# Two-block network on one core: fourteen modulation sums moved out of the keys-and-values stage into the attention blocks, by halves, and the transposes of the context's roots moved two row tiles ahead

## The chip, the cores and the metric

One Trainium2 chip, of which the program uses 1 core. The time is device microseconds of one execution; lower is better. It was taken in three runs before the change, and one further execution was recorded by the profiler.

## The reference, cut to what matters

The network has two blocks. The part that the change touches is the first layer of the first block, attention over 512 latent tokens and 256 context tokens, and the modulation vector that feeds it:

```python
m_lat = (s_c @ ada_w[l] + ada_b[l])[:, None, :]          # 6*1024 sums over 1024
sh1, sc1, g1, sh2, sc2, g2 = jnp.split(m_lat, N_MOD, axis=-1)
h_lat = modulate(rms_norm(x, mix_norm[l]), sh1, sc1)
h_ctx = modulate(rms_norm(ctx, mix_norm[l]), csh1, csc1)
y_lat, y_ctx = attention_mixer(h_lat, h_ctx, ...)
x = x + g1 * y_lat
x = x + g2 * conv_ffn(modulate(rms_norm(x, ffn_norm[l]), sh2, sc2), ...)
...
# attention_mixer: keys and values of context and latent tokens side by side
p = (p1 - lam * p2)                     # 4 differential heads, two softmaxes each
oa = rms_norm(einsum(p, v), subln) * (1 - lam_init)
ob = gqa_attend(rms_norm(qb), rms_norm(kb), vb)          # 8 grouped query heads
```

`sh1` and `sc1` are wanted before attention; `g1`, `sh2` and `sc2`, of which the change moves sums, only after it.

## The kernel before, in words

All products are done in float32 split into a high and a low part, so each product of two tiles is three matmuls (lines 205 to 207); the high part is written by ScalarE (line 160, `wh`, `kh`, `vah`, `reg`, `pth`), the low part by VectorE (lines 163 and 169, `wl`, `kl`, `val`, `ptl`). Weights arrive as `raw` tiles of 128x1024 through the queue of SyncE, two buffers deep in this stage, and are split into one of three `wh`/`wl` pairs.

A modulation vector of 1024 is eight columns of 128 in `mod`. Each column is one load of a 128x1024 tile `ada` (512 KB) and one VectorE instruction, a product with the vector `silu_c` and a sum along the row (line 454, shown as CUSTOM_DVE_ANT_0, followed by a read of the accumulator).

The stages around the change, in the order of the program:

- **Row tiles** (`attention1_start`): a schedule written out by hand for all engines. For each of eight row tiles of x, VectorE and ScalarE write `h` (lines 1054 to 1057), then TensorE multiplies what is there with six weight tiles (`tiles`, two in single banks `b1`, four in the two double banks `b2`). At k == 4 VectorE works out the roots of the context's mean squares (`A`, tile `spread`); at k == 7 TensorE transposes them into `Rc`, a piece of bank `side`. After the eight tiles VectorE forms the context's rows from `cx` and `Rc`.
- **Keys and values** (`attention1`, up to `self.lam()`): rope of four query tiles and two key tiles (lines 714 to 717), the stores of keys, the products for values (`v_copy`, `v_all`) and for three more key tiles, each for latent and context tokens (`kv_gemm`). `more(2)` puts two modulation sums after each step, fourteen in all, with two `ada` buffers. There are two single banks; a product waits until VectorE and ScalarE have read the bank's last content. `lam()` loads a small vector on ScalarE's queue (`lv`), sums it on VectorE and takes an exponential on ScalarE (line 989). In this stage the builder's scheduler sets each engine's order; engines work their queues in that order.
- **Blocks of attention**: the order of TensorE is written out by hand, the others follow the scheduler. Blocks 0 to 15 are those of the differential heads, with two score products, two maxima (`nm`, line 910), two exponentials (`e`, line 914) and two GpSimd instructions (lines 964 and 965) each; blocks 16 to 47 are those of the grouped heads, with one of each and no GpSimd. Two blocks later the weights are transposed (line 926) and split (`pth`, `ptl`), then multiplied with the values. Between them, `fill()` puts steps of the remaining projections: four query tiles in bank `side` (`q_norm_steps`), with their norms on VectorE (`hn_v`, `hn_y`, `rsq_b`, `spread`, `hn`) and, once, the norm and store of the last key tile `k` through two `e` tiles. There are four `e` tiles, and scores have two double banks, freed by the exponential.
- **Output** (`attention1_out`): the remaining ten sums of the layer, unchanged.

Of the kernel before, what the change touches and what calls it, by code (L numbers as in the profile page):

```python
# [9 lines left out]
F32 = mybir.dt.float32  # L10
# [3 lines left out]
ALU = mybir.AluOpType  # L14
# [4 lines left out]
P = 128  # L19
# [100 lines left out]
class Net:  # L120
# [331 lines left out]
    def ada_tile(self, pool, l, m, tag, bufs):  # L452
        r = self.ada_raw(pool, l, m, tag, bufs)
        self.nc.vector.tensor_tensor_reduce(  # L454
            out=r, in0=r, in1=self.silu_c, scale=1.0, scalar=self.col("ada_b", 48 * l + m), op0=ALU.mult, op1=ALU.add,
            accum_out=self.mod[:, l, m:m + 1])

    def ada_start(self, rows, pairs):

# [535 lines left out]
    def attention1_start(self, es, hc):  # L995


        nc = self.nc
# [4 lines left out]
        with self.tc.manual_schedule(engines=FULL_ORDER):  # L1003
# [70 lines left out]
            for k in range(KD):  # L1074
                r = rows(x[k], k, 0, R, h[0][k], h[1][k])
# [27 lines left out]
                if k == 4:  # L1103
                    A = root(stc, 1024.0)
                next(s)
                if k == 7:
                    self.spread_rows(A, 2, Rc)

                for z in tiles:
# [8 lines left out]
            for k in range(KD):  # L1118
                c = tuple(self.t(hc, [P, NCTX], F32R, f"c{n}{k}") for n in "hl")
                self.hctx.append(c)  # L1120
                r = rows(cx[:, k, :], k, 1, Rc, *c)
# [12 lines left out]
    def attention1(self):  # L1134
        nc = self.nc
        with ExitStack() as es:
# [3 lines left out]
            with ExitStack() as e0:  # L1140
                hc = self.adap = self.pool(e0, "hc")
                with ExitStack() as e1:
                    qs, ks = self.attention1_start(e1, hc)
                kvp = self.pool(e0, "kvp")
                inp = self.pool(es, "inputs", side="right")
                ada = iter(range(16, 40))

                def more(n):
                    for _ in range(n):
                        self.ada_tile(kvp, 0, next(ada), "ada", 2)  # L1150

                for s, z in enumerate(ks):
                    self.k_store(kvp, *z, s, nc.vector)
                    more(2)
                vt = self.v_copy(kvp, 13)
                more(2)
                self.v_all(kvp)
                more(2)
                for s, w in enumerate((5, 7)):
                    self.k_store(kvp, *self.kv_gemm(w), 2 + s, nc.vector)  # L1160
                    more(2)
                self.v_store(kvp, vt, 4)
                more(2)
                key = [self.t(inp, [P, 768], F32, "k16"), self.t(kvp, [P, 768], F32, "vt", 1)]
                bc, bl = self.kv_gemm(12)
                self.gained(None, bc, self.col("k_norm"), None, 0, key[0][:, 0:NCTX], key[1][:, 0:NCTX])
                squares = self.gained(None, bl, self.col("k_norm"), None, 0, key[0][:, NCTX:], key[1][:, NCTX:])[2]
                hv = self.t(self.tiny, [P, 28], F32, "hn_v", 2)
                self.mean_sq(hv[:, 16:28], key[1], 64.0, 1e-6, self.sel2)
                with self.tc.issue_after(squares.ins):  # L1170
                    self.lam()
            ap = self.adap = self.pool(es, "attn")
# [7 lines left out]
            q, k, v, es_, pts = {j: [] for j in range(6)}, {}, {}, {}, {}  # L1180
# [34 lines left out]
            with self.tc.manual_schedule(engines=PE_ORDER):  # L1215
                for n in range(max(due) + 2):
                    if n < len(blocks):
                        m, i, qt = blocks[n]
# [12 lines left out]
                        pts[due[n]] = pt  # L1231
                    if n < len(blocks):
                        rest()
                    if n == 40:
                        hn = self.new_h(0)
                    if 40 <= n < 46:
# [3 lines left out]
                    if j % 2:  # L1240
                        m, i, qt = blocks[j]
                        at = slice((qt - 1) * P, (qt + 1) * P)
# [618 lines left out]
```

## Time and profile before

| | |
|---|---|
| median of 3 runs | 3438.53 us (3437.78 to 3439.02) |
| profiled execution, its own time | 3439.95 us |
| its span, first to last instruction | 3438.2 us |
| TensorE busy (share of the span) | 3323.4 us (97%) |
| VectorE busy | 1994.2 us (58%) |
| ScalarE busy | 1379.2 us (40%) |
| GpSimd busy | 291.6 us (8%) |
| mean granted TensorE clock | 0.986 |

Times in the trace are microseconds from the span's start. PE is TensorE, DVE VectorE, ACT ScalarE, POOL GpSimd, SP SyncE. The change lies in the first 400 us; from 394 us on TensorE is busy for 2992.31 of 3044 us. The idle time before an instruction is given in brackets with what ended it; where the engine named had long been done, it was another.

### The profile page before, as it was taken

The page shows a single profiled execution, that of the slowest core. Times are in us where ns is not written, and L with a number is a line of the kernel's source. Part 1 is how long each engine was busy: PE and PEld are TensorE (multiplying, and loading weights), DVE is VectorE, ACT ScalarE, POOL GpSimd, SP SyncE. Part 2 cuts the span into 40 slices and gives each one's busy share as a digit, 9 for nine tenths or more (in the row PEclk, how much of TensorE's full clock was granted, in tenths as well). Part 3 has the DMA queues.
Part 4 walks back from the last instruction along what each step waited for, and adds up shares of the span by engine and source line. Part 5 has one row for each costly group of instructions (what it writes and reads, how often), then busy time and mean ns, then how long its engine had stood idle before and what let it go on. Part 6 is the DMA issues. An engine that isn't in the chain of part 4 may idle for free.

```text
span 3438.2 us, 43735 instructions
## 1 busy us (share of the span) xinstructions
PE 3323.4 (97%) x17013; PEld 2847.3 (83%) x17013; DVE 1994.2 (58%) x3406; ACT 1379.2 (40%) x2085; POOL 291.6 (8%) x341
## 2 busy tenths in 40 slices
PE   8878999999999999999999999999999999899998
PEld 7767798888888889888888888898888888788887
DVE  6777887766574555333776533363333699873335
ACT  3246643334353343222485522242222466552222
POOL 0052000000000000000222100020000222220001
PEclk9989999999999999999999999999999999999999
DMA  5731456643232323222222323245222133133231
GB/s 196 244 109 34 181 167 204 206 144 102 74 104 98 99 84 104 95 97 93 76 93 89 105 97 98 93 136 185 97 94 93 50 104 99 43 119 98 91 101 47
DMA packets 126209, 381.74 MB, mean 111 GB/s; under 512 B 13745, under 2 KB 28209, under 8 KB 125874
## 3 DMA queue, kind: packets, MB, share of 16 engines
q1 hardware_dynamic: 125282, 377.77, 33.9%
q8 instruction: 134, 2.20, 0.3%
q10 hardware_dynamic: 720, 1.18, 0.1%
q14 instruction: 73, 0.60, 0.1%
HBM read 360.54 MB, written 18.35 MB: 110 GB/s over the span
## 4 chain that ended last, share of the span: by engine, by line
PE 85%; DVE 6%; ACT 4%; issue 3%; DMA 2%; POOL 1%; SPq 0%; ACTq 0%; DVEq 0%; POOLq 0%
PE b L205 23%; PE b L207 23%; PE b L206 23%; PE side L205 2%; PE b L88 1%; PE bo L942 1%; PE side L206 1%; PE side L207 1%; PE b L85 1%; PE b L86 1%; PE b L926 1%; DVE wl L163 1%; PE s L834 1%; PE s L833 1%; DVE nm L910 1%
## 5 line engine op out<-in xcount | busy, mean ns | idle before, releaser
L205 PE MATMUL b<-reg,wh 128*128 128x512 f32 (+1 forms) x3841 | 1435.5, 375 | 16.1 <-ACT wh L160 5.6
L206 PE MATMUL b<-reg,wh 128*128 128x512 f32 (+1 forms) x3841 | 1435.5, 374 | 2.3 <-DVE reg L163 2.3
L207 PE MATMUL b<-reg,wl 128*128 128x512 f32 (+1 forms) x3841 | 1434.6, 374 | 0.5 <-DVE wl L163 0.5
L160 ACT ACTIVATE wh<-raw 128x1024 fp32r<-128x1024 f32 (+2 forms) x549 | 559.7, 1026 | 1318.0 <-PE b L206 1178.8
L163 DVE TENSOR_TENSOR wl<-raw,wh 128x1024 fp32r<-128x1024 f32 (+2 forms) x549 | 653.2, 1195 | 557.8 <-ACT wh L160 549.0
L205 PEld LDWEIGHTS b<-reg,wh 128*128 128x128 f32 x3841 | 727.1, 189 | 145.3 <-ACT wh L160 6.0
L206 PEld LDWEIGHTS b<-reg,wh 128*128 128x128 f32 x3841 | 727.1, 189 | 129.7 <-DVE reg L163 2.7
L207 PEld LDWEIGHTS b<-reg,wl 128*128 128x128 f32 x3841 | 726.8, 189 | 128.9 <-DVE wl L163 1.0
L696 DVE TENSOR_TENSOR sg<-sg,b 128x512 f32<-128x512 f32 x88 | 60.4, 688 | 283.2 <-PE b L207 275.3
L617 POOL TENSOR_TENSOR accs<-x,x 128x512 f32<-128x512 f32 x6 | 10.3, 1709 | 2447.3 <-DVE x L615 2447.3
L1695 DVE SCALAR_TENSOR_TENSOR x<-b,x 128x512 f32<-128x512 f32 x64 | 44.3, 692 | 190.1 <-PE b L207 190.1
L85 PE MATMUL b<-reg,wh 128*128 128x256 f32 x496 | 126.8, 288 | 7.1 <-ACT reg L656 6.5
L86 PE MATMUL b<-reg,wl 128*128 128x256 f32 x496 | 124.8, 284 | 0.0
L530 ACT ACTIVATE sq<-x 128x256 f32<-128x256 f32 (+1 forms) x111 | 51.6, 472 | 162.9 <-DVE x L608 88.0
L160 ACT ACTIVATE reg<-sg 128x512 fp32r<-128x512 f32 x132 | 83.1, 630 | 73.2 <-DVE sg L701 70.9
L454 DVE CUSTOM_DVE_ANT_0 ada<-ada,silu_c,cols 128x1024 f32<-128x1024 f32 x80 | 99.2, 1280 | 12.4 <-DMA ada<-ada 12.4
L160 ACT ACTIVATE pth<-b 128x384 fp32r<-128x384 f32 (+1 forms) x160 | 82.0, 534 | 59.1 <-PE b L926 56.4
L205 PE MATMUL side<-reg,wh 128*128 128x512 f32 x221 | 98.1, 444 | 6.2 <-DVE hn L755 3.9
L85 PEld LDWEIGHTS b<-reg,wh 128*128 128x128 f32 x496 | 95.5, 192 | 9.2 <-ACT reg L656 8.4
L163 DVE TENSOR_TENSOR ptl<-b,pth 128x384 fp32r<-128x384 f32 (+1 forms) x160 | 94.5, 603 | 14.5 <-ACT pth L160 13.5
L163 DVE TENSOR_TENSOR reg<-sg,reg 128x512 fp32r<-128x512 f32 x132 | 90.3, 685 | 18.2 <-ACT reg L160 18.2
L926 PE MATMUL b<-ident,e 128*128 128x128 f32 x544 | 83.4, 282 | 15.2 <-DVE ptl L163 7.9
(356 smaller groups left out, 4031.1 us busy)
## 6 DMA issues: line engine op xcount, KB each, us to landing
raw<-up SPq DMA_DIRECT2D x264, 512.0 KB, 3.4
ada<-ada SPq DMA_DIRECT2D x88, 512.0 KB, 5.0
raw<-down SPq DMA_DIRECT2D x96, 448.0 KB, 3.3
raw<-down SPq DMA_DIRECT2D x48, 512.0 KB, 3.3
raw<-q SPq DMA_DIRECT2D x24, 512.0 KB, 3.4
raw<-rg_in SPq DMA_DIRECT2D x20, 512.0 KB, 3.3
raw<-attn_in SPq DMA_DIRECT2D x14, 512.0 KB, 5.8
raw<-rg_out SPq DMA_DIRECT2D x16, 320.0 KB, 3.0
```

The source lines that it names most:

```text
L85: mm(out=b[:, sl], lhsT=w[0][:, k, :], rhs=h, start=k == 0, stop=False)
L86: mm(out=b[:, sl], lhsT=w[1][:, k, :], rhs=h, start=False, stop=False)
L160: return self.nc.scalar.activation(out=hi, in_=src, func=AF.Copy, scale=scale)
L163: return self.nc.vector.tensor_tensor(out=lo, in0=src, in1=hi.bitcast(F32), op=ALU.subtract)
L205: mm(out=ps, lhsT=ah, rhs=bh, start=first, stop=False)
L206: mm(out=ps, lhsT=ah, rhs=bl, start=False, stop=False)
L207: mm(out=ps, lhsT=al, rhs=bh, start=False, stop=last)
L454: self.nc.vector.tensor_tensor_reduce(out=r, in0=r, in1=self.silu_c, scale=1.0, scalar=self.col("ada_b", 48 * l + m), op0=ALU.mult, op1=AL ...
L530: self.nc.scalar.activation(out=s, in_=x, func=AF.Square)
L696: nc.vector.tensor_tensor(out=sg, in0=sg, in1=bu, op=ALU.mult)
L926: nc.tensor.transpose(out=b[:, i * P:(i + 1) * P], in_=e[:, (k0 + i) * P:(k0 + i + 1) * P], identity=self.ident)
L1695: self.nc.vector.scalar_tensor_tensor(out=x[m], in0=b, scalar=c, in1=x[m], op0=ALU.mult, op1=ALU.add)
```

## The change

The call `more(2)` goes, and with it the fourteen sums after the steps of keys and values. A new helper loads half a column's tile (128x512, 256 KB) and sums it; the second half starts from the first one's result, and there is one buffer. The source places one half in each block n from 17 to 44, 28 halves. The transposes of the context's roots go from k == 7 to k == 5.

```diff
+    def ada_half(self, pool, l, m, half):
+        r = self.t(pool, [P, 512], F32, "ada", 1)
+        at = slice(512 * half, 512 * half + 512)
+        nc.sync.dma_start(out=r, in_=self.a["ada"][48 * l + m][:, at])
+        acc = self.mod[:, l, m:m + 1]
+        nc.vector.tensor_tensor_reduce(out=r, in0=r, in1=self.silu_c[:, at], scale=1.0,
+                                       scalar=acc if half else self.col("ada_b", 48 * l + m), op0=ALU.mult, op1=ALU.add, accum_out=acc)
...
-                if k == 7:
+                if k == 5:
                     self.spread_rows(A, 2, Rc)
...
-                def more(n):
-                    for _ in range(n):
-                        self.ada_tile(kvp, 0, next(ada), "ada", 2)
...
                 for s, z in enumerate(ks):
                     self.k_store(kvp, *z, s, nc.vector)
-                    more(2)
                 vt = self.v_copy(kvp, 13)
-                more(2)
                 self.v_all(kvp)
-                more(2)
                 for s, w in enumerate((5, 7)):
                     self.k_store(kvp, *self.kv_gemm(w), 2 + s, nc.vector)
-                    more(2)
                 self.v_store(kvp, vt, 4)
-                more(2)
...
                     if n < len(blocks):
                         rest()
+                    if 17 <= n < 45:
+                        if n % 2:
+                            part = next(ada)
+                        self.ada_half(ap, 0, part, 1 - n % 2)
```

Lines from 464 on carry a number ten higher after the change, in `attention1` too up to the removed calls. What the builder makes of it, at three places:

TensorE in the row tiles: `ident,spread` are the two transposes of the context's roots, `reg` the rows of h, `silus,ada` the last small products of the modulation. Before, 60 rows after these products:

```order
L205 MATMUL b_82_210<-reg_5_52_141,ada_544 128x512
L206 MATMUL b_82_210<-reg_13_60_149,ada_544 128x512
L207 MATMUL b_82_210<-reg_5_52_141,ada_545 128x512
L382 MATMUL side_153<-ident_78,spread_467 128x128 x2
L205 MATMUL b_104_292<-reg_6_53_142,wh_288 128x512
```

and after it, directly behind them:

```order
L206 MATMUL b_81_209<-reg_11_58_147,wh_411 128x512
L207 MATMUL b_81_209<-reg_3_50_139,wl_412 128x512
L494 MATMUL bo_154<-silus_157,ada_484 128x2 x8
L382 MATMUL side_153<-ident_78,spread_467 128x128 x2
L205 MATMUL b_104_292<-reg_4_51_140,wh_288 128x512
```

The transposes moved ahead of the products of row tiles 4 and 5.

ScalarE at the end of keys and values: `k` and `vt` are the copies of the last key tile's banks (128x512 latent, 128x256 context), `lv` the load of lam's vector, `misc` its exponential, `e` the first softmax. Before:

```order
L731 ACTIVATE k_262_1271<-b_267_1279,cols_76 128x512
L732 ACTIVATE vt_1272<-b_267_1279 128x512
L983 DMA lv_1342<-lam 128x256
L160 ACTIVATE wh_1524<-raw_1522 128x1024
L731 ACTIVATE k_262_1271<-b_268_1280,cols_76 128x256
L732 ACTIVATE vt_1272<-b_268_1280 128x256
L989 ACT_TABLE_LOAD
L989 ACTIVATE misc_90<-misc_90 128x2
L914 ACTIVATE e_1396,zs_1365<-b_293_1389,nm_1394 128x768
```

and after:

```order
L741 ACTIVATE k_248_1229<-b_253_1237,cols_76 128x512
L742 ACTIVATE vt_1230<-b_253_1237 128x512
L993 DMA lv_1300<-lam 128x256
L999 ACT_TABLE_LOAD
L999 ACTIVATE misc_90<-misc_90 128x2
L160 ACTIVATE wh_1482<-raw_1480 128x1024
L741 ACTIVATE k_248_1229<-b_254_1238,cols_76 128x256
L742 ACTIVATE vt_1230<-b_254_1238 128x256
L924 ACTIVATE e_1354,zs_1323<-b_279_1347,nm_1352 128x768
```

The exponential of lam moved ahead of a weight's split and of the two context copies.

VectorE in block 7 of the differential heads: `nm` are its two maxima, `rsq_b`, `hn_y` and `spread` the last Newton step of the norms and its spreading, `rz` a softmax's weight. Before:

```order
L362 SCALAR_TENSOR_TENSOR rsq_b_1682<-rsq_b_1682,hn_v_1333 128x28
L163 TENSOR_TENSOR ptl_1739<-b_389_1746,pth_1738 128x3x128
L363 SCALAR_TENSOR_TENSOR hn_y_1681<-rsq_b_1682,hn_y_1681 128x28
L962 RECIPROCAL rz_1754<-z_1729 128x1
L747 COPY spread_1779<-hn_y_1681 128x256
L963 SCALAR_TENSOR_TENSOR rz_1754<-rz_1754,zs_1365,misc_90 128x1
L910 TENSOR_REDUCE nm_1802<-b_399_1797 128x1
L910 TENSOR_REDUCE nm_1811<-b_403_1806 128x1
```

and after:

```order
L920 TENSOR_REDUCE nm_1760<-b_385_1755 128x1
L973 SCALAR_TENSOR_TENSOR rz_1712<-rz_1712,zs_1323,misc_90 128x1
L363 SCALAR_TENSOR_TENSOR hn_y_1639<-rsq_b_1640,hn_y_1639 128x28
L465 ISA ada_2816,mod_86<-ada_2816,silu_c_159,mod_86 128x512
L465 ISA mod_86 128x1
L920 TENSOR_REDUCE nm_1769<-b_389_1764 128x1
L361 TENSOR_TENSOR rsq_b_1640<-hn_y_1639 128x28
L362 SCALAR_TENSOR_TENSOR rsq_b_1640<-rsq_b_1640,hn_v_1291 128x28
L363 SCALAR_TENSOR_TENSOR hn_y_1639<-rsq_b_1640,hn_y_1639 128x28
L757 COPY spread_1737<-hn_y_1639 128x256
```

A half (the two ISA rows) stands between the two maxima, and the spread moved from ahead of both maxima to behind them. VectorE's queue is not in the hand-written order, and the scheduler puts the first half behind block 0 and the last one into block 18.

## Rows read from the trace of the kernel before

**Rows 1.** Busy time by stretch: us, busy of each engine, granted clock, DMA share, GB/s.

```profile
85.86:176.00 90.14, 79.87 (x394) 67.81 (x394) 62.03 (x101) 24.21 (x37) 0.00 (x0) 0.92 0.81 249
176.00:205.00 29.00, 26.01 (x141) 22.30 (x142) 17.66 (x34) 17.36 (x36) 14.05 (x8) 0.94 0.42 127
205.00:245.00 40.00, 24.02 (x133) 20.55 (x132) 35.97 (x64) 17.02 (x38) 23.88 (x15) 0.80 0.27 79
245.00:276.00 31.00, 30.26 (x177) 26.53 (x177) 18.43 (x32) 17.33 (x37) 18.48 (x12) 0.93 0.28 77
276.00:303.00 27.00, 19.12 (x124) 16.92 (x122) 24.01 (x47) 15.46 (x34) 12.77 (x8) 0.89 0.18 59
```

**Rows 2.** TensorE in order of time: start, us, line, out<-in; idle before, and its end.

```profile
81.98 0.40 PE L207 MATMUL b<-reg,wl 128*128 128x512 f32 x1
...
87.81 0.36 PE L205 MATMUL b<-ch,wh 128*128 128x256 f32 x1 [1.95 <-DVE tmp L715]
...
98.67 0.50 PE L205 MATMUL b<-reg,wh 128*128 128x512 f32 x1 [3.54 <-DVE kl L169]
```

**Rows 3.** VectorE in order of time, from the context's rows to the first key's low part.

```profile
77.54 0.87 DVE L1054 SCALAR_TENSOR_TENSOR tmp<-cx,ga,side 128x256 f32<-128x256 f32 x2 [11.13 <-PE side L382]
...
85.21 0.74 DVE L714 STREAM_SHUFFLE tmp<-b 128x512 f32<-128x512 f32 x1
...
98.20 0.76 DVE L169 SCALAR_TENSOR_TENSOR kl<-b,kh 128x256 fp32r<-128x256 f32 x2
```

**Rows 4.** VectorE: a modulation sum that waits for its load.

```profile
152.57 1.28 DVE L454 CUSTOM_DVE_ANT_0 ada<-ada,silu_c,cols 128x1024 f32<-128x1024 f32 x1 [4.77 <-DMA ada<-ada]
```

**Rows 5.** TensorE: latent product of key 7, its context product, then the same of key 12.

```profile
155.23 0.77 PE L205 MATMUL b<-reg,wh 128*128 128x512 f32 x1 [4.77 <-DVE tmp L715]
...
163.29 0.28 PE L205 MATMUL b<-ch,wh 128*128 128x256 f32 x1
...
166.70 0.48 PE L205 MATMUL b<-reg,wh 128*128 128x512 f32 x1
...
172.28 0.28 PE L205 MATMUL b<-ch,wh 128*128 128x256 f32 x1
```

**Rows 6.** VectorE: an instruction of 512 columns, then a sum of 1024.

```profile
101.30 0.69 DVE L715 TENSOR_TENSOR tmp<-b,rc 128x512 f32<-128x512 f32 x1
101.90 1.28 DVE L454 CUSTOM_DVE_ANT_0 ada<-ada,silu_c,cols 128x1024 f32<-128x1024 f32 x1
```

**Rows 7.** ScalarE at the end of keys and values (ACTq: its DMA queue).

```profile
172.49 0.33 ACTq L983 DMA_DIRECT2D lv<-lam  x1
...
175.19 1.06 ACT L160 ACTIVATE wh<-raw 128x1024 fp32r<-128x1024 f32 x1 [1.54 <-PE b L206]
...
176.52 0.37 ACT L732 ACTIVATE vt<-b 128x256 f32<-128x256 f32 x1
...
179.12 0.20 ACT L989 ACTIVATE misc<-misc 128x2 f32<-128x2 f32 x1 [0.93 <-DVE misc L988]
```

**Rows 8.** VectorE, then TensorE, at the same place.

```profile
178.39 0.36 DVE L987 TENSOR_TENSOR lv<-lv 128x64 f32<-128x64 f32 x2 [0.28 <-DMA lv<-lam]
...
176.94 1.50 PE L370 MATMUL side<-sel,vt 128*128 128x2 f32 x12 [0.96 <-ACT vt L732]
```

**Rows 9.** DMA issues: KB each, median us from issue to landing.

```profile
kscr<-e SPq DMA_DIRECT2D x2, 384.0 KB, 2.3
```

**Rows 10.** GpSimd, then VectorE twice the same operation, in blocks 5 to 7.

```profile
207.32 1.87 POOL L965 TENSOR_TENSOR e<-e,e 128x768 f32<-128x768 f32 x1
...
208.28 0.95 DVE L362 SCALAR_TENSOR_TENSOR rsq_b<-rsq_b,hn_v 128x28 f32<-128x28 f32 x1
...
212.08 0.17 DVE L362 SCALAR_TENSOR_TENSOR rsq_b<-rsq_b,hn_v 128x28 f32<-128x28 f32 x1
```

**Rows 11.** TensorE in blocks 9 and 10 of the differential heads.

```profile
233.57 0.80 PE L833 MATMUL b<-kk,reg 128*128 128x512 f32 x1 [7.83 <-ACT e L914]
...
243.34 0.80 PE L205 MATMUL side<-reg,wh 128*128 128x512 f32 x1 [3.88 <-DVE hn L755]
```

More of the change, by code (lines that the diff above doesn't have):

```diff
@@ L456, in ada_tile @@
             accum_out=self.mod[:, l, m:m + 1])
+    def ada_half(self, pool, l, m, half):
+        nc = self.nc
+        r = self.t(pool, [P, 512], F32, "ada", 1)
[4 more added lines that the diff above has]
+                                       scalar=acc if half else self.col("ada_b", 48 * l + m), op0=ALU.mult, op1=ALU.add, accum_out=acc)
     def ada_start(self, rows, pairs):
```

## The prediction

> **What bounds the kernel now.** I read the busy times by stretch first [rows 1], then TensorE's idle times, then who ended them. To 85.86 us TensorE runs without a gap from the row tiles on, and from 394 us on it is 98% busy, so only 86 to 394 us can change. In keys and values (85.86 to 176) TensorE is busy 79.87 of 90.14 us and VectorE 62.03: here TensorE sets the time, except in three waits of 1.95, 3.54 and 4.77 us [rows 2, 5]. In the differential blocks it changes twice: from 176 to 205 and from 245 to 276 TensorE is busy 26.01 of 29 and 30.26 of 31 us, with VectorE at 17.66 and 18.43; from 205 to 245 and from 276 to 303 VectorE is busy 35.97 of 40 and 24.01 of 27 us, and TensorE only 24.02 and 19.12. The chain there runs through maximum, exponential, next score. Where the 28 halves land counts more than how many they are. By the order of the changed kernel, counted against the maxima, 7 stand in 176 to 205, 8 in 205 to 245, 8 in 245 to 276 and 5 in 276 to 303: most lie in the differential heads, which have GpSimd beside them, and not in the grouped ones.
>
> **Roots.** Two transposes stand elsewhere, none is added. In the old place VectorE stood idle for 11.13 us until they came [rows 3]; the roots themselves were ready long before, so TensorE need not wait for them in the new place. The context's rows are then done before the first of the six tiles is. What follows is bound by the next limit: TensorE needs a single bank free. The first tile's last product ends at 82.38 (81.98 + 0.40) [rows 2], while TensorE has other tiles' products up to 85.86 (87.81 - 1.95), and shuffle and rope of that tile take some 1.3 us, so the wait of 1.95 goes. The second wait, 3.54, hangs on the first `kl` in VectorE's queue. Before, 12.99 us lay between the first shuffle (85.21) and that `kl` (98.20) [rows 3]. In the new order the same piece of queue has one more 512-wide operation (0.60 from start to start [rows 6]), one more `wl` (about 1.1, as twice the columns) and two fewer context rows (some 0.4 each): 13.9 us. From 82.4 that gives 96.3, so TensorE starts 1.9 us sooner than at 98.67, not 5.5. **Term: -1.9**, bounds 0 (if splits stand in the way, nothing is left) and -5.5 (both waits go).
>
> **Sums out of keys and values.** Removed from VectorE are 14 sums of 1.28 us [rows 6], 17.9 us, and 14 loads of 512 KB from SyncE's queue at a DMA share of 0.81 [rows 1]. TensorE has the time, so all but one wait was hidden: the last sum but one stood 4.77 us waiting for its load with the shuffle and rope of key 5 behind it [rows 4], and TensorE waited 4.77 us for that bank [rows 5]. Without it the rope runs during key 5's context product. The wait had an aftermath: the 24 products that followed took 8.06 us (155.23 to 163.29), the same 24 for key 12 took 5.58 (166.70 to 172.28) [rows 5]; behind the gap the first product takes 0.77 us, for key 12 it takes 0.48, since the granted clock is at the lower of its two levels (1.2 and 2.4 GHz). The 2.48 us go as well. **Term: -4.77 - 2.48 = -7.25**, bounds -4.8 (the clock falls anyway) and -7.3.
>
> **Lam on ScalarE.** The new order puts lam's exponential ahead of a split and of the copies `k`, `vt` of the context bank, for which TensorE waits (`sel,vt`). Queued behind the waiting exponential are one `wh`, `k`, `vt` and the first softmax. Before, the load was issued at 172.49, used by VectorE at 178.39, and the exponential ran at 179.12, 2.2 us after `vt` had released TensorE at 176.94 [rows 7, 8]. After, the issue comes 0.7 us later (a score of four products stands ahead of key 12), at 173.2. If the load takes 2.3 us, as 384 KB do on a quiet queue [rows 9], it lands at 175.5; if it takes as before, 5.9, at 179.1. From landing to the end of `vt` it is 0.75 (178.37 to 179.12), 0.1 for the exponential, then from the start of the split to the end of `vt` 1.7 (175.19 to 176.89) [rows 7]: 2.6 us. TensorE goes on at 178.1 to 181.7 instead of 176.94. With fewer loads and the stores of values earlier the queue should be half empty, so I take the middle. **Term: +3**, bounds 0 (the following products hide it) and +7.2 (4.7, and the clock falls for 2.5 as after the gap of 4.77).
>
> **The 28 halves.** No 512-wide sum is in the trace. A 512-wide operation runs 0.69 us and lets the next start after 0.60; half of the 1024-wide sum is 0.64 [rows 6]. With the read of the accumulator I take 0.68, between 0.60 and 0.77. In 176 to 205 and 245 to 276 that is 4.8 and 5.4 us against 11.3 and 12.6 us in which VectorE is idle [rows 1]: nothing, since TensorE has the time there (up to 3 if the halves stand in wrong places). In 205 to 245, 8 x 0.68 = 5.4 us go into a queue with 4.0 us of idle time, which itself is waiting for an exponential; I take **+5.4**. In 276 to 303, 5 x 0.68 = 3.4 against 3.0: **+3.4**. Low bounds: -2.4 and 0.4. The first, since the new order on ScalarE lets block 8's first exponential run ahead of the key's copy into an `e` tile, which may shorten the wait of 7.83 us by one place; the second is 3.4 less the idle 3.0. High bounds +9.4 and +5.4, with GpSimd (below). A half's load waits in SyncE's queue for the sum before it (one buffer), with the next head's keys and values behind it; these are loaded a head ahead, so I price that at nothing.
>
> **Sum:** -1.9 - 7.25 + 3 + 5.4 + 3.4 = +2.65 on the span of 3438.2, 3440.9. The profiled execution took 3439.95, 1.4 more than the median of 3438.53; the change goes on the median: **3441.2 us**.
>
> **What GpSimd does to a half.** A VectorE operation of 28 columns took 0.17 us alone and 0.95 at 208.28, where it ended at 209.23 with the GpSimd instruction that had run since 207.32 and ended at 209.19 [rows 10]. A maximum, which reads a bank, is not held. The sum reads two tiles of SBUF, and no row of before shows one beside GpSimd. The Trainium skill, page "SBUF — State Buffer", section "Who interferes with whom", says that a VectorE instruction with two SBUF inputs and a GpSimd instruction that reads SBUF exclude each other, the later one waiting until the earlier is through; by that every half is held, and holds GpSimd in turn, and the time is that of the first rival. The row at 208.28 agrees with it for a smaller operation.
>
> **Rivals.**
> - *GpSimd's turn comes in between (slower).* GpSimd is busy 23.88 of 40 us in 205 to 245 and 12.77 of 27 in 276 to 303 [rows 1]. A half that meets an instruction of 1.87 waits 0.9 on average: 8 x (0.68 + 0.6 x 0.85) = 9.4 and 5 x (0.68 + 0.47 x 0.85) = 5.4. Sum -9.15 + 3 + 14.8 = +8.6: 3447. It decides from 1.04 us a half on (13 x 1.04 = 13.5, total +7). For it: rows 10. Against it: part of such waits would have met the next operation anyway.
> - *All is covered (faster).* The scheduler placed halves where VectorE would be idle; the wait of 7.83 breaks up [rows 11], lam lands early. -9.15 + 1.1 + 0 + 0.4 = -7.65: 3430.9. For it: 28 x 0.68 = 19 us against 31 us of idle time in 176 to 303. Against it: the two stretches where TensorE waits for VectorE (3.88 for `hn` [rows 11]), and the spread now behind both maxima.
> - *Lam's load stays slow.* +7.2 in place of +3: +6.85, 3445.4.
> - *The roots' move does nothing:* the waits behind the ropes remain whole; +4.55, 3443.1.
>
> **How the numbers follow.** Forecast 0.45, GpSimd 0.20, covered 0.17, lam 0.08, roots 0.10. What a measurement of this kernel can tell from no change is about 0.2%, 6.9 us: below 3431.7 faster, above 3445.4 slower. Faster is the covered case, 0.17. Slower is the GpSimd case and half of lam, 0.24. The same is the rest, 0.59. All low bounds together give -14.8 (-5.5 - 7.3 + 0 - 2.4 + 0.4), all high ones +20 (0 - 4.8 + 7.2 + 9.4 + 5.4 + 3). They will not fall together; a range from the covered case to a little over the GpSimd case, 3430.5 to 3449.5, leaves some 2 in 10 out.
>
> **What the new profile would show.** Roots: VectorE's idle time before the context's rows is gone, TensorE's wait of 1.95 too, and one of some 3 us stays before the `kl`. Sums: no wait of 4.77 behind key 5, and the next 24 products in 5.6 us. Lam: ScalarE idle before line 999, TensorE waiting 2 to 6 us before `sel,vt`. Halves: sums of 0.6 to 0.75 us without GpSimd, of over 1 beside it, TensorE idle longer than before in the two VectorE stretches. I am wrong if the stretch from block 5 to block 10 takes less than before, if the sums stand where TensorE has the time, or if anything after the attention changes by more than a microsecond.

## The result, and the profile after

The changed kernel takes 3461.05 us (median; 3458.81 to 3463.63) against 3438.78 us of the kernel before in the same comparison: ratio 1.0063, 95% interval 1.0052 to 1.0075, that is 18 to 26 us slower. The prediction was 3441.2 with a range to 3449.5. It is slower, and outside the range.

What went as foretold stands ahead of the differential blocks. The profile after, TensorE in order of time (start, duration, line, operation, idle time before it and what ended it):

```profile
96.67 0.80 PE L205 MATMUL b<-reg,wh 128*128 128x512 f32 x1 [5.46 <-DVE kl L169]
...
149.75 0.48 PE L205 MATMUL b<-reg,wh 128*128 128x512 f32 x1
...
155.31 0.40 PE L843 MATMUL b<-kk,reg 128*128 128x512 f32 x1
...
171.00 2.72 PE L370 MATMUL side<-sel,vt 128*128 128x2 f32 x12 [3.68 <-ACT vt L742]
```

The wait of 1.95 us in [rows 2] is gone as such, but the one behind it has grown from 3.54 to 5.46 us; the one of 4.77 in [rows 5] is gone. Key 7's 24 latent products run from 149.75 to 155.31, 5.56 us; in [rows 5] they took 8.06 behind the gap. The wait for `vt` is 3.68 in place of 0.96 [rows 8].

What the change costs stands behind that. The same view after, in the differential blocks:

```profile
211.01 0.50 PE L843 MATMUL b<-kk,reg 128*128 128x512 f32 x1 [4.08 <-ACT e L924]
...
224.98 0.69 PE L763 MATMUL side<-ident,spread 128*128 128x128 f32 x2 [6.12 <-DVE spread L757]
...
244.15 0.79 PE L843 MATMUL b<-kk,reg 128*128 128x512 f32 x1 [9.46 <-ACT e L924]
...
270.31 0.80 PE L843 MATMUL b<-kk,reg 128*128 128x512 f32 x1 [4.73 <-ACT e L924]
...
301.23 0.80 PE L843 MATMUL b<-kk,reg 128*128 128x512 f32 x1 [5.74 <-ACT e L924]
```

The large waits for an exponential were one of 7.83 us [rows 11] and are now four of 4 to 9.5, and a fifth wait stands before a spread. Busy time by stretch, after (columns as in [rows 1]: us, TensorE, its weight loads, VectorE, ScalarE, GpSimd, granted clock, DMA share, GB/s):

```profile
171.00:200.00 29.00, 25.51 (x111) 21.60 (x112) 17.54 (x34) 11.31 (x23) 12.58 (x7) 0.77 0.37 112
200.00:245.00 45.00, 24.01 (x147) 21.52 (x146) 36.33 (x73) 17.30 (x39) 22.05 (x14) 0.82 0.45 126
245.00:285.00 40.00, 31.46 (x146) 26.89 (x146) 28.72 (x49) 15.48 (x33) 20.31 (x12) 0.74 0.39 112
285.00:330.00 45.00, 33.47 (x190) 29.71 (x189) 39.37 (x76) 23.02 (x50) 17.31 (x10) 0.82 0.22 76
```

VectorE has idle time in all of them, so its busy share alone doesn't explain the loss. Waits explain most of it. From the third maximum to the 33rd (counted below) the kernel after takes 122.9 us and the kernel before 100.2. TensorE's idle time there is 38.6 in place of 21.6 us, 17.0 more; the other 5.7 us are the same 444 matmuls, which take longer at a mean granted clock of 0.81 in place of 0.88. The waits from 170 us on; engine, waiting operation, releaser, total us, times, longest:

```profile
DVE ada L465 <- DMA ada<-ada: 20.3, 16, 3.1
...
ACT e L924 <- DVE nm L920: 32.1, 12, 7.1
...
PE b L843 <- ACT e L924: 24.4, 5, 9.5
```

VectorE stands 20.3 us waiting for the loads of halves; ScalarE waits for VectorE's maxima (32.1 us, 26.5 before); TensorE waits for ScalarE's exponentials, 24.4 us in place of 10.2. Two halves and a third, VectorE in order of time, with the group of DMA issues they wait for (KB each, median us from issue to landing):

```profile
204.53 0.75 DVE L465 CUSTOM_DVE_ANT_0 ada<-ada,silu_c,mod 128x512 f32<-128x512 f32 x1 [3.06 <-DMA ada<-ada]
...
208.12 0.75 DVE L465 CUSTOM_DVE_ANT_0 ada<-ada,silu_c,cols 128x512 f32<-128x512 f32 x1 [1.82 <-DMA ada<-ada]
...
211.55 1.57 DVE L465 CUSTOM_DVE_ANT_0 ada<-ada,silu_c,mod 128x512 f32<-128x512 f32 x1 [0.66 <-DMA ada<-ada]
```

```profile
ada<-ada SPq DMA_DIRECT2D x28, 256.0 KB, 2.7
```

There is one buffer, so a load goes out only when the sum before it has ended, and lands 2.6 to 5.7 us after its issue, 2.7 in the median. Where two halves stand closer than that, everything behind the second waits. The half at 211.55 shows the second cost: 1.57 us in place of 0.74. So two causes are on the table, the loads and GpSimd. Ten halves took 1.4 to 2.2 us, 10.8 us more than at 0.74.

### The profile page after: what moved, and what is told of

The parts are those of the page before. It is cut to its first block, busy times and chain, and to the rows that moved or that the text cites. A ratio compares the mean times of both kernels' runs of the same rounds, so it can differ in the third digit from the quotient of the medians.

```text
span 3458.2 us, 43787 instructions
## 1 busy us (share of the span) xinstructions
PE 3326.7 (96%) x17013; PEld 2850.5 (82%) x17013; DVE 2004.6 (58%) x3434; ACT 1379.6 (40%) x2085; POOL 293.0 (8%) x341
## 4 chain that ended last, share of the span: by engine, by line
PE 80%; DVE 6%; ACT 3%; issue 3%; DMA 2%; POOL 0%; ACTq 0%; POOLq 0%; DVEq 0%; SPq 0%
PE b L205 23%; PE b L207 23%; PE b L206 23%; DMA ada<-ada 2%; PE b L88 1%; PE bo L952 1%; PE b L85 1%; PE b L86 1%; PE side L205 1%; PE side L206 1%; PE side L207 1%; PE b L936 1%; DVE nm L920 1%; DVE ada L465 1%; PE s L844 1%
## 5 line engine op out<-in xcount | busy, mean ns | idle before, releaser
L936 PE MATMUL b<-ident,e 128*128 128x128 f32 x544 | 85.6, 286 | 17.8 <-DVE ptl L163 10.8
L163 DVE TENSOR_TENSOR ptl<-b,pth 128x384 fp32r<-128x384 f32 (+1 forms) x160 | 94.6, 603 | 11.8 <-ACT pth L160 10.6
L936 PEld LDWEIGHTS b<-ident,e 128*128 128x128 f32 x544 | 67.4, 147 | 33.9 <-DVE ptl L163 10.3
```

Of the source, the lines that this page charges most:

```text
L163: return self.nc.vector.tensor_tensor(out=lo, in0=src, in1=hi.bitcast(F32), op=ALU.subtract)
L936: nc.tensor.transpose(out=b[:, i * P:(i + 1) * P], in_=e[:, (k0 + i) * P:(k0 + i + 1) * P], identity=self.ident)
```

## Experiments

Each kernel was compared with the kernel before on the same chip; times in text are medians, ratios have their 95% interval. One thing had to be learned first. TensorE's row tiles don't last equally long in every execution: in the profiles of after and of six kernels below that leave this part as it is, the first key product starts anywhere from 92.5 to 96.7 us. So stretches of the trace are compared between two maxima and not from the start. VectorE's maxima are 64 in number, 32 in the differential blocks. For keys and values the stretch runs from the end of the row tiles, which is the end of the last product ahead of the first context product (`ch`), to maximum 3. Read from each profile:

| kernel | us, row tiles' end to maximum 3 | maximum 3 to 33 | 33 to 64 | 3 to 64 | ratio |
|---|---|---|---|---|---|
| before | 97.6 | 100.2 | 100.4 | 200.6 | 1 |
| roots only | 102.9 | 100.2 | 100.2 | 200.4 | 1.0002 |
| after | 94.5 | 122.9 | 103.7 | 226.6 | 1.0063 |
| no halves | 94.4 | 100.1 | 99.7 | 199.7 | 0.9986 |
| one input, one buffer | 95.3 | 111.7 | 103.1 | 214.9 | 1.0036 |
| loads three deep | 96.1 | 109.9 | 99.9 | 209.8 | 1.0019 |
| one input, three buffers | 95.1 | 99.9 | 99.6 | 199.5 | 0.9980 |
| halves without loads | 95.0 | 106.9 | 104.0 | 210.9 | 1.0025 |
| halves in grouped | 95.0 | 100.6 | 118.7 | 219.3 | 1.0042 |
| lam's load early, no halves | 92.3 | 100.7 | 100.2 | 200.8 | 0.9992 |
| mix | 97.0 | 106.7 | 101.8 | 208.5 | 1.0020 |
| ten and fourteen | 96.3 | 100.1 | 100.2 | 200.2 | 1.0003 |
| twelve and twelve | 100.2 | 100.0 | 100.2 | 200.2 | 1.0006 |
| ten and fourteen, held | 96.8 | 98.3 | 103.5 | 201.8 | 1.0000 |

The blocks can be cut at the maxima nearest to the prediction's stretches (maxima 11, 21, 31 and 37 come at 205.8, 246.3, 280.5 and 302.3 us before). The second column is what the prediction gave the halves there:

| maxima | predicted for the halves | no halves | after | loads three deep | one input, one buffer | one input, three buffers |
|---|---|---|---|---|---|---|
| 3 to 11, TensorE's | 0 | 22.2 | 28.9 | 23.6 | 26.8 | 23.0 |
| 11 to 21, VectorE's | +5.4 | 40.5 | 45.6 | 45.4 | 43.9 | 40.6 |
| 21 to 31, TensorE's | 0 | 34.2 | 44.6 | 35.7 | 37.4 | 31.9 |
| 31 to 37, VectorE's | +3.4 | 22.1 | 25.7 | 25.4 | 23.9 | 23.9 |

**Without the halves** (label no_halves).

```
-                        self.ada_half(ap, 0, part, 1 - n % 2)
-                ada = iter(range(16, 40))
+                ada = iter(range(30, 40))
```

> The kernel after without the 28 halves: the fourteen sums are left out, and their columns of the modulations are zero. It gives what the rest of the change is worth, and so the price of the halves. At 176 us the trace of after was 5.9 us ahead of before, so if nothing else in it costs time: 3433 (3429 to 3435), and the halves cost 28 us in all. Rival (the differential blocks became slower for another reason, lam on ScalarE or the key's copy behind an exponential): over 3440, and the halves cost less than 20.

Measured: 3435.29, ratio 0.9986 (0.9977 to 0.9996), 1.4 to 7.9 us faster than before. The rest of the change is a gain, and from maximum 3 to 64 the blocks take what they took before. The whole loss is the halves: 226.6 - 199.7 = 26.9 us. The rival falls.

**Roots alone** (roots_only).

```
-                if k == 7:
+                if k == 5:
                     self.spread_rows(A, 2, Rc)
```

> The kernel before with nothing but the two transposes of context's roots put two row tiles sooner; the fourteen sums stay in keys and values. Theory of the prediction (roots -1.9 us by themselves, the loss is all in the halves): 3436 to 3438 us against 3438.8 of before, TensorE's wait of 1.95 us gone. Rival (the sooner start of the key products is given back, because the sums of keys and values still stand 4.77 us behind their load, which comes no sooner): 3438 to 3440, with that wait longer by what was won.

Measured: ratio 1.0002 (0.9993 to 1.0012). TensorE's waits in keys and values, a sum of VectorE ahead of the first of them, and the stretches there (columns as above):

```profile
PE b L205 <- DVE val L163: 6.6, 1, 6.6
...
PE side L370 <- ACT vt L732: 3.4, 1, 3.4
...
143.72 1.28 DVE L454 CUSTOM_DVE_ANT_0 ada<-ada,silu_c,cols 128x1024 f32<-128x1024 f32 x1 [5.58 <-DMA ada<-ada]
...
85.00:130.00 45.00, 39.54 (x197) 33.36 (x196) 37.73 (x61) 11.85 (x18) 0.00 (x0) 0.92 0.77 239
130.00:180.00 50.00, 40.03 (x203) 34.08 (x202) 24.28 (x41) 15.25 (x24) 0.00 (x0) 0.91 0.99 275
```

The rival's time holds. The first key product does start sooner, 11.1 us after the end of the row tiles in place of 12.8, but what follows takes it back. The wait of 4.77 for key 5's rope is gone, and one of 6.6 us stands in its place some 10 us earlier, before a product that waits for a value's low part; again it stands behind a sum that waited for its load, 5.58 us. From 130 on the DMA share is 0.99 (0.97 before). A second wait has grown too, that for `vt`, from 0.96 to 3.4 us. Which of the two decides was not separated; in this profile they make the stretch to maximum 3 even longer than before, 102.9 against 97.6 us.

**Three buffers for the loads** (loads_three_deep).

```
-        r = self.t(pool, [P, 512], F32, "ada", 1)
+        r = self.t(pool, [P, 512], F32, "ada", 1) if (2 * m + half) % 3 == 0 \
+            else self.t(self.small, [P, 512], F32, "sq", 2)
...
+                        with self.tc.issue_after(self.nms[AT[n - 17] - 1]):
+                            self.ada_half(ap, 0, part, 1 - n % 2)
```

> The kernel after, every half behind the same maximum as there, but with three buffers for their loads in place of one (two are tiles of the norms that lie idle in attention). What goes is the wait of VectorE for a half's load, 20.3 us in 16 waits in the trace of after; the sums and GpSimd beside them stay. Theory load (that wait is the larger part of the loss): 3440 to 3446. Theory GpSimd (the halves stretched to 1.4 to 2.2 us, 10.8 us in ten of 28, and all that waits behind them make the loss): 3455 to 3461.

Measured: 3446.47, ratio 1.0019 (1.0010 to 1.0029). VectorE waits for no load of a half any more, and 16.8 of the 26.9 us are gone. The load theory gave the right size (half a us over its range), but 10.1 us are left. They stand beside GpSimd. GpSimd and VectorE of this kernel, in order of time:

```profile
264.83 1.80 POOL L977 TENSOR_TENSOR e<-e,e 128x768 f32<-128x768 f32 x1
```

```profile
265.25 1.93 DVE L466 CUSTOM_DVE_ANT_0 sq<-sq,silu_c,cols 128x512 f32<-128x512 f32 x1
...
267.22 0.75 DVE L466 CUSTOM_DVE_ANT_0 ada<-ada,silu_c,mod 128x512 f32<-128x512 f32 x1
```

GpSimd's add ends at 266.63, the half at 267.18, 0.55 later. The next half, with GpSimd idle, takes 0.75.

**The same with one input** (one_input).

```
-        nc.vector.tensor_tensor_reduce(out=r, in0=r, in1=self.silu_c[:, at], scale=1.0, ...)
+        nc.vector.tensor_reduce(out=acc, in_=r, axis=AX.X, op=ALU.add)
```

> The kernel with loads three deep, but each half only adds up the 512 columns of its loaded tile, without the product with the modulation input (that product is left out): one tile of SBUF is read in place of two, and the loads and the places in VectorE's queue stay. In the kernel with loads three deep eleven halves took 1.2 to 1.9 us in place of 0.74, 8.2 us in all. Theory of the prediction's GpSimd rival (a VectorE instruction that reads two tiles of SBUF takes turns with GpSimd, one that reads a single tile does not): no half over 0.8 us, and the time falls from 3446.5 to 3439 to 3443. Rival (bare work in VectorE's queue makes the rest of the loss, and GpSimd only lengthens what would have waited anyway): no half over 0.8, but 3444 to 3447. Third (whatever reads SBUF on VectorE takes turns with GpSimd): halves of 1.2 to 1.9 stay, 3445 to 3448.

Measured: 3431.28, ratio 0.9980 (0.9971 to 0.9989). The same place in this kernel, GpSimd and VectorE:

```profile
252.74 1.81 POOL L976 TENSOR_TENSOR e<-e,e 128x768 f32<-128x768 f32 x1
```

```profile
253.16 0.68 DVE L466 TENSOR_REDUCE mod<-sq 128x1 f32<-128x512 f32 x1
...
253.87 0.69 DVE L466 TENSOR_REDUCE mod<-ada 128x1 f32<-128x512 f32 x1
```

The half starts 0.42 us into GpSimd's add, as the other did, and takes 0.68. From maximum 3 to 64 the kernel takes 199.5, as without halves. Both rivals fall: this sum over one tile isn't held, and the bare work of 28 sums in VectorE's queue costs nothing in the differential blocks, in this order. No half took over 0.69 us. The time lies even below what the theory named, since I had left bare work in it. The edit makes a half shorter in the queue too, 0.59 in place of 0.67 us from start to start; these 28 x 0.08 = 2.2 us were not separated from the 10.1.

The Trainium skill, page "SBUF — State Buffer", section "Who interferes with whom", says that a VectorE instruction with two SBUF inputs contends with a GpSimd instruction that reads SBUF, and that one with at most one SBUF input, outside the 2-port modes, doesn't. Both runs agree with it: 1.93 and 0.68 us beside the same GpSimd instruction.

**One input and one buffer** (one_input_one_buffer), the square's last corner: the edit of one_input with the buffer of the kernel after.

> The kernel after with its one buffer for the loads, each half behind the same maximum, but a half only adds up its 512 loaded columns (the product with the modulation input is left out). With loads three deep and one_input it fills the square of one or three buffers, two tiles read or one. From maximum 3 to maximum 33 the profiles gave 122.9 us (one buffer, two tiles), 109.9 (three buffers, two tiles), 99.9 (three buffers, one tile), 100.1 (no halves). If the load wait and the turns with GpSimd are two causes that add up: 99.9 + 13 = 113 us there, 3444 to 3450, ratio 1.001 to 1.003. Rival (the waits for loads are only there because stretched halves hand the buffer on late): under 104 us there, 3433 to 3438.

Measured: 3450.78, ratio 1.0036 (1.0023 to 1.0049), a little over the expected range; 111.7 us from maximum 3 to 33 against 113 expected. VectorE still waits for loads:

```profile
DVE mod L466 <- DMA ada<-ada: 14.8, 14, 2.8
```

The causes add up. Over 199.7 (no halves), from maximum 3 to 64: the loads alone 214.9 - 199.7 = 15.2 us, two inputs alone 209.8 - 199.7 = 10.1, both 26.9, which is 1.6 more than the sum.

**Without loads** (halves_without_loads).

```
-        nc.sync.dma_start(out=r, in_=self.a["ada"][48 * l + m][:, at])
-        ... in0=r, in1=self.silu_c[:, at] ...
+        ... in0=self.silu_c[:, at], in1=self.silu_c[:, at] ...
```

> The kernel after, every half behind the same maximum as there, but its sum runs over the modulation input in SBUF times itself and nothing is loaded (the sums are left out as such). No load, no wait for one, no load in SyncE's queue ahead of the next head's keys. Theory load: like the kernel with loads three deep within 2 us, 3439 to 3446, since only the wait counted. Theory GpSimd: 3455 to 3461. A third (the loads take DMA time from keys and values of the next head): 3 us or more under the kernel with loads three deep.

Measured: 3447.2, ratio 1.0025 (1.0016 to 1.0035), a little over the expected range, and 210.9 us from maximum 3 to 64 against 209.8 with three buffers. So the transfers as such cost nothing, only the wait for them; the third theory falls.

**Halves held to the grouped heads** (halves_in_grouped).

```
+                        with self.tc.issue_after(self.last_nm.ins):
                             self.ada_half(ap, 0, part, 1 - n % 2)
```

> The kernel after with loads three deep and each half held behind the maximum of its own block, so that all 28 run in the grouped heads, where GpSimd does nothing. There VectorE is busy 18.1 of 20 us from 340 to 380 and 12.8 of 17 and 17 of 20 before that. Theory bare work (a half of 0.74 in a queue with 10% of idle time delays the next split): 28 x 0.66 = 18.5 us into some 13 us of idle time of which half is of use: 3440 to 3447. Theory GpSimd (only the neighbourhood of GpSimd makes halves dear): 3435 to 3438.

Measured: 3451.64, ratio 1.0042 (1.0028 to 1.0055), more than either theory gave. Three of the 28, ahead of 300 us, still ran beside GpSimd and took 0.92 to 1.64 us, the others 0.73 to 0.75. From maximum 33 to 64 it takes 118.7 in place of 99.7 us, 19.0 more. Two stretches of it with halves, and the first of them again in the kernel without:

```profile
340.00:360.00 20.00, 14.73 (x104) 12.61 (x102) 19.89 (x43) 13.85 (x30) 0.00 (x0) 1.00 0.24 79
360.00:380.00 20.00, 16.21 (x116) 14.17 (x117) 19.89 (x43) 14.32 (x33) 0.00 (x0) 1.00 0.29 93
```

```profile
340.00:360.00 20.00, 18.52 (x136) 16.36 (x134) 18.09 (x33) 16.48 (x37) 0.00 (x0) 1.00 0.00 1
```

With halves VectorE is full. Without them it was busy 18.09 of 20 us and TensorE 18.52, so both looked alike; the halves show that VectorE's round of maximum and split sets the pace there. Its idle tenth was used up first: from maximum 46 to 63, where GpSimd does nothing, the 16 halves add 10.6 us to VectorE's busy time (49.00 in place of 38.43) and 7.2 to the stretch (49.4 in place of 42.3). The 12 ahead of them cost 11.9 us, 1.0 each, with a granted clock of 0.79 in place of 0.88. So that 19.0 is 28 x 0.68 is a coincidence.

**Lam's load early** (lam_load_early), on the kernel without halves.

```
+                self.lv = self.t(self.adap, [P, 256], F32, "lv")
+                nc.scalar.dma_start(out=self.lv, in_=self.a["lam"].broadcast_to([P, 256]))
                 vt = self.v_copy(kvp, 13)
```

> The kernel without halves (their sums left out), with the load of lam's vector put ahead of the first value product, and nothing else. In the kernel without halves VectorE waits 6.29 us for that load and TensorE 3.7 us for vt behind the exponential that waits for it. If the lam term of the prediction is right (+3 us): that wait falls to under 1 us, 3431 to 3433 against 3435.3. Rival (what follows is bound by the first exponentials and takes the time again): 3434 to 3436.

Measured: 3435.45, ratio 0.9992 (0.9983 to 1.0001), no gain, and so inconclusive on the size of the term. The wait for `vt` fell from 3.7 to 1.7 us. But the scheduler had put the load among those of the input. The view of the tile lv (issue, then what VectorE waited for, us and times) and TensorE's first row tile:

```profile
L1160 ACTq DMA_DIRECT2D lv<-lam x1: 334/334/334, 4.7 to 4.7; - x1
...
  DMA lv<-lam: 4.2, 1
```

```profile
33.58 0.77 PE L205 MATMUL b<-reg,wh 128*128 128x512 f32 x1
```

It was issued at 4.7 us, VectorE waited 4.2 us for it at the start, and the first row tile began at 33.58; without the edit it begins at 32.25. From the row tiles' end to maximum 3 it takes 92.3 in place of 94.4 us, 2.2 less, and from there to maximum 64 it gives 1.1 back (200.8 in place of 199.7), which speaks for the rival. That is one profile, and the median shows neither.

**Attempts at a kernel that beats both.** The mix has ten sums in keys and values and four as eight halves:

```
+AT = (2, 6, 6, 17, 17, 20, 25, 25)
...
-                    if 17 <= n < 45:
+                    if 17 <= n < 25:
...
                 self.v_all(kvp)
+                more(4)
```

> An attempt at a kernel that beats both: roots as after, ten of the fourteen sums again in keys and values, four as eight halves with loads three deep behind maxima after which VectorE is idle for 1 to 3 us (in the first differential head, and in the third and fourth), lam's vector loaded early. If the loss is load waits and VectorE work in the wrong stretches: within 2 us of the kernel without halves, less what the early lam gives: 3432 to 3437, ratio 0.998 to 0.9995. Rival (the last two of the ten sums wait for their loads again as in the kernel before, and TensorE for the bank behind them): 3438 to 3441.

Measured: 3444.89, ratio 1.0020 (1.0010 to 1.0030), more than either expectation. It loses 208.5 - 199.7 = 8.8 us in the blocks. Its halves explain little of that: five of the eight took 0.74 or 0.75 us, the other three 0.95 to 1.42. But two of them in a row stand ahead of the third head's spread and key, and these then meet GpSimd. GpSimd and VectorE of the mix:

```profile
232.69 1.47 POOL L976 TENSOR_TENSOR e<-e,rz 128x768 f32<-128x768 f32 x1 [0.18 <-DVE rz L975]
```

```profile
226.29 0.74 DVE L466 CUSTOM_DVE_ANT_0 sq<-sq,silu_c,cols 128x512 f32<-128x512 f32 x1
...
227.57 0.42 DVE L758 COPY spread<-hn_y 128x512 f32<-128x512 f32 x1
...
233.04 1.40 DVE L758 COPY spread<-hn_y 128x512 f32<-128x512 f32 x1
...
236.26 1.52 DVE L170 SCALAR_TENSOR_TENSOR e<-tmp,e 128x512 fp32r<-128x512 f32 x1
...
240.53 0.16 DVE L974 RECIPROCAL rz<-z 128x1 f32<-128x1 f32 x1 [2.75 <-ACT e L926]
```

The copy at 233.04 reads one tile and is held all the same: 1.40 us beside GpSimd, 0.42 without. From maximum 17 to 19 the mix takes 18.4 us and the kernel without halves 15.1, from 25 to 27 12.0 and 8.4. So a place where VectorE waits for an exponential is not a free place; which of the delays there decides was not settled.

The other kernels have no sum in the blocks; ten or twelve stand in keys and values, the rest in the output product:

```
+                ada = iter([*range(16, 26), *range(32, 40), *range(26, 32)])
...
                     self.ada_tile(ap, 0, m, "ada", 4)
+                    if m == 39:
+                        self.gain(0, 1)
```

> No sum in the attention blocks: roots as after, lam's vector loaded early, the first ten of the fourteen sums in keys and values, the other four behind those that stand in the output product anyway (the scales first, so that the gain is not later than before, then the shifts). Keys and values: the wait for key 5's rope falls from 4.8 us to under 2 (1.9 in the mix, which has the same ten), nothing in the blocks: 4 to 6 us won by the first maxima. The output product: four sums of 1.28 us on a VectorE that is 63 to 99% busy there, and four loads of 512 KB at a DMA share of 1.02 until 414 us. Theory (these are hidden, since TensorE has the time there and the shifts are needed after 438 us): 3433 to 3437, ratio 0.998 to 0.9995. Rival (the loads come late in the output product, behind them its weights): 3439 to 3443.

Measured: 1.0003 (0.9994 to 1.0012). TensorE's waits in keys and values, then in the output product:

```profile
PE b L205 <- DVE tmp L715: 1.9, 1, 1.9
...
PE norm L370 <- DVE acc L531: 2.7, 1, 2.7
```

The first was 4.8 before and is 1.9, as expected; but of the 4 to 6 us that were to be won by the first maxima, the stretch to maximum 3 shows only 1.4 (96.3 against 97.6 us). The second wait is new: two sums stood ahead of the last squares. Lam's load was at the start here too.

> As the kernel with ten and fourteen, but twelve sums in keys and values (one each behind the last two keys) and twelve in the output product. If keys and values are bound by the loads of the last sums: TensorE waits 3 to 5 us for key 5's rope and the time is that of before within 2 us, 3437 to 3441. If the two more loads find room: 2 us under the kernel with ten and fourteen where that loses in the output product, else the same.

Measured: 1.0006 (0.9997 to 1.0015). The wait in keys and values is back, at 7.1 us: two more loads of 512 KB are enough.

In the last kernel lam's load is held behind a weight split and the last two sums stand behind the norm's roots:

```
+                with self.tc.issue_after(self.last_hi.ins):
+                    nc.scalar.dma_start(out=self.lv, in_=self.a["lam"].broadcast_to([P, 256]))
...
+                    if n == 1 and sl.start == 0:
+                        for m in self.ada_left[-2:]:
+                            self.ada_tile(ap, 0, m, "ada", 4)
```

> The kernel with ten and fourteen with its two losses mended. Lam's load stood there at 4.6 us among the loads of the input, and the first row tile began at 33.6 in place of 32.3 us; it is now held behind a weight split in keys and values. And two sums stood ahead of the last squares in the output product, for which TensorE waited 2.7 us before the norm; the last two shifts are now summed behind the norm's roots, where VectorE was idle 1.5 us and the product goes on. Theory (both were what ate the gain of keys and values): first row tile at 32.3, no wait of 2.7, 3434 to 3437, ratio 0.9985 to 0.9995. Rival (the start varies by itself, and the output product loses elsewhere what it wins there): 3438 to 3440, ratio 0.9996 to 1.0005.

Measured: 1.0000 (0.9991 to 1.0009). The first row tile begins at 32.24 and the wait before the norm is 0.7, so both were mended, but the time is that of before: the rival. Without any of the fourteen sums only 1.4 to 7.9 us are to be had. In this kernel's profile keys and values win 0.9 us to maximum 3, the blocks lose 1.2 (201.8 against 200.6) and all that stands behind maximum 64 loses 1.8 (3055.9 against 3054.1); why the last two lose was not found. No kernel that computes everything beats the kernel before.

## Why the prediction was wrong

**Roots, -1.9.** Right in the start of the key products, and by the chain that was named: from the end of the row tiles it is 11.1 us in every profile with the roots moved and was 12.8 before, 1.7 sooner. Wrong in the waits: TensorE waits as long as before (5.46 in one wait, 1.95 + 3.54 in two), where one of some 3 us was to stay. The gain is that the context products, no longer behind a gap, take 5.8 in place of 7.3 us (0.28 us each in place of up to 0.42). Alone it won nothing: in roots_only what follows took it back, since the loads of the sums stand there and the wait for `vt` grew. The term is no sum of its own; it counts at most together with the next one.

**Sums out of keys and values, -7.25, and lam, +3.** Right in the waits: the 4.77 and its aftermath went, the wait for `vt` grew by 2.7 us. Too good as a sum. With the roots the three made -6.15; no_halves measured 1.4 to 7.9 us faster, and to maximum 3 its profile shows 3.2 (94.4 against 97.6 us). Where the other 3 us went is not settled. Behind the wait for `vt` the granted clock was 0.72 from 174 to 180 us in no_halves and 1.00 in the kernel before, and the prediction had a lower clock there only in the upper bound of lam's term. With lam's load early 2.2 us more are won, about what is taken off the wait (3.7 to 1.7), and the clock there is 0.72 all the same.

**The 28 halves, +8.8: the failed step.** They cost 26.9 us from maximum 3 to 64. By stretch it is 5.1 and 3.6 us in the two of VectorE, where 5.4 and 3.4 were priced, and 6.7 and 10.4 in the two of TensorE, which were priced at *"nothing, since TensorE has the time there"*. TensorE's time there did not help: in after it waits there for norms and exponentials (3.22 us up to 189.73, 4.73 up to 270.31, 5.74 up to 301.23) that VectorE handed on late, behind the halves. Where the number is right it is so by luck: with the loads in time and one tile read, 11 to 21 takes 40.6 us in place of 40.5. Three things in that step were wrong.

- *"A half's load waits in SyncE's queue for the sum before it (one buffer) ... so I price that at nothing."* I asked who is queued behind the load on SyncE's queue and not who waits for the load itself: the next sum, in VectorE's queue, with the maxima behind it. This is the term that decided, 15.2 us by itself; with two tiles read, three buffers take 5.3 and 8.9 us off TensorE's stretches, and 0.2 and 0.3 off VectorE's. It could have been worked out: [rows 9] had a load of 384 KB at 2.3 us, and by the order six pairs of halves stood behind one maximum each, closer together than a load takes: in the kernel with three buffers, where nothing holds them, two of them start at 201.80 and 202.95.
- *GpSimd, at a chance of 0.20.* The mechanism was right and was read from the right row [rows 10]; that part of the waiting would have met the next operation anyway was wrong. I priced it at 6 us on top of bare work for 13 halves (14.8 - 8.8); alone it costs 10.1 for all 28. The sum was a little off too: 8 x (0.68 + 0.6 x 0.85) is 9.5 and not 9.4.
- *Bare work, +5.4 and +3.4.* With the loads in time and one tile read it is zero: one_input has all 28 sums of one tile at 0.67 to 0.69 us and runs as without them. So the part that I priced was free, and the two that I left out or held unlikely made the loss. That 205 to 245 and 276 to 303 were full of VectorE work [rows 1] was no proof that more of it would delay the end.

The range failed for the same reason: its upper end took the GpSimd case for the worst, and no case had the load wait. "If the sums stand where TensorE has the time" was among the things that would prove me wrong. Fifteen of them did stand there, as the order had shown, and they cost the most.

The scheduler is a part of it. The code has the halves in blocks 17 to 44, most of them grouped heads; nothing held them there, and they were issued from the first differential block on, as the prediction had read from the order. But halves_in_grouped shows that the place in the code would have cost 19.0 us too.

## What to carry to other kernels

A load with one buffer in front of an engine's in-order queue must be priced as a wait of that engine: take the time from issue to landing and compare it with the distance between the two users, at the closest pair and not on the average. Then ask of each VectorE instruction moved beside GpSimd how many of its inputs lie in SBUF; with two, count GpSimd's remaining time into its own, and for a copy of one tile too (1.40 in place of 0.42 us in the mix). And the busy share of two engines that are both near 90% doesn't tell which one has time to spare: only work added to one of them, with nothing else changed, did.

## What the hardware showed that was not expected

A narrow operation takes these turns too. In the kernel with one input a VectorE operation on one column, whose inputs both lie in SBUF, took 1.25 us beside GpSimd and 0.22 without it. GpSimd, then VectorE twice:

```profile
238.44 1.64 POOL L726 TENSOR_TENSOR tmp<-tmp,rs 128x512 f32<-128x512 f32 x1 [2.32 <-DVE tmp L724]
```

```profile
238.85 1.25 DVE L974 SCALAR_TENSOR_TENSOR rz<-rz,zs,misc 128x1 f32<-128x1 f32 x1
...
245.38 0.22 DVE L974 SCALAR_TENSOR_TENSOR rz<-rz,zs,misc 128x1 f32<-128x1 f32 x1
```

It ended at 240.10, GpSimd's instruction at 240.08. GpSimd pays as well, here less than VectorE does: its second rope operation, mean ns of one between 165 and 340 us, without halves, with loads three deep, and with one input:

```profile
L728 POOL TENSOR_TENSOR tmp<-tmp,tmp 128x512 f32<-128x512 f32 x5 | 6.8, 1352 | 0.2
```

```profile
L728 POOL TENSOR_TENSOR tmp<-tmp,tmp 128x512 f32<-128x512 f32 x5 | 7.9, 1578 | 0.3
```

```profile
L727 POOL TENSOR_TENSOR tmp<-tmp,tmp 128x512 f32<-128x512 f32 x5 | 6.8, 1358 | 0.3
```

Also unexpected: TensorE's row tiles, in which it is never seen idle, ended up to 4 us apart in executions of kernels with the same code there. Why was not looked into. A term of 2 us can't be read from the start of one profile for that reason; counted from the end of the row tiles it can, as the 11.1 and 12.8 us show.
